# Gate values in two blocks of 512 columns, the norm weights' row spread by TensorE, and the head's steps in a new order

## The chip, the cores and the metric

The kernel runs on one core of a Trainium2 chip. The metric is device time in microseconds (us), the median of the runs. The profile is that of one execution, with every instruction's start and length; its engines are PE (TensorE matmul), PEld (its weight loads), DVE (VectorE), ACT (ScalarE), POOL (GpSimd) and SP, which only issues transfers.

## The reference

Two layers on x of 1024 tokens by 1024, all float32. The first is a chunked spatial gate, the second a Mamba-2 mixer, then a last norm. The change lies in the first layer, up to its third part v:

```python
hn = rmsnorm(h, norm_w[0])                        # h: 1024 x 1024
z, u, v = jnp.split(hn @ w_in, 3, axis=-1)        # w_in: 1024 x 6144, each part 2048 wide
v = layernorm(v, ln_w, ln_b)
mixed = jnp.einsum('gts,bcsgd->bctgd', w_causal, v.reshape(..., 8, 256)) + b_s   # 8 groups of 256 columns
h = h + (u * mixed * jax.nn.silu(z)) @ w_out
```

## The kernel before

Every float32 matmul is made of three on split operands: a value is rounded to `fp32r` (the high half, made by ACT as a rule), the rest is the low half (made by DVE), and `mm3` (lines 134 to 136) adds high x high, high x low and low x high into one accumulator in PSUM. Products of 1024-deep matrices are made by a scheme of Strassen's kind: x's transpose is cut into four quarters A11, A12, A21, A22 of 512 by 512, a block of weights into b[kh, j], and seven products replace eight. Besides quarters they take sums of them: of x S1 to S4 (lines 398 to 431), of the weights t1 = b01 - b00, t2 = b11 - t1, b10 - t2 and b11 - b01.

`Block` is one such block of weights. For the gate values v (`v_block`, line 328) a block is two groups of 256 columns (j = 0, 1), so there are four blocks; the stationary operand is a 128x128 piece of x's quarter, the moving one 256 columns of weights, and a product is two units of two halves of 4 x 3 matmuls. `done` adds what was kept of earlier products (`u`), writes 128 x 2 x 256 to `v_d` in DRAM and takes the layer norm's statistics (`bn_stats`).

`head` (line 351) is the start. Its order is written out by hand (`tc.manual_schedule`): each engine does its instructions in the order in which the code names them. For each of x's eight rows of 128 tokens: load (`load_x`), sum of squares on ACT (`sq`), the root (`rs_a`, a power on POOL; `rs_b`, a correction on DVE), scale and norm weights on DVE (`norm`, line 381; the weights `nwb` are loaded broadcast to 128 partitions), eight transposes on TensorE (`tr`, 387), and then copies and halves. Between them stand the seven products of the first block (`blk.mm`) and the start of the second. Sums of x rows are made on DVE (`sums(V, ...)`) or by a transfer through POOL's queue that adds into its target (`sums(None, ...)`, `blk.add`).

Behind the head the rest of the second block, the mixing weights (lines 560 to 586: transposes of `ws`, a matmul with `ones`) and blocks three and four follow, ordered by a scheduler. Small loads (`hv`, `dsk`, lines 594 to 606) stand in the code behind them; the scheduler put them early. `dsk` is read in single values: 64 copies of 16 values that lie two apart, twice. Then eight groups g of z and u follow (`Block` with 512 moving columns of x), whose first matmul is the first one that reads as `acc<-hh,wh`. Tiles come from pools with a fixed number of slots: `s8` 16, `q4` 8, `k2` 4 (the outputs `vt` and the mixing weights `wc` share them), `wr` 4, `wh` and `wl` 3; a tile waits until its slot is free.

Of the kernel before, what the change touches and what calls it, by code (L numbers as in the profile page):

```python
# [8 lines left out]
F32 = mybir.dt.float32  # L9
# [13 lines left out]
G = 8  # L23
# [6 lines left out]
def kernel(  # L30
# [297 lines left out]
    def v_block(gp):  # L328
        def done(name, i, a, b):
            th, j = int(name[1]) - 1, int(name[2]) - 1  # L330
            g = 2 * gp + j
            vt = k2([P, 2, 256], "vt")
            vf = vt.rearrange("p a b -> p (a b)")
            if b is None:
                nc.scalar.copy(out=vf, in_=a)
            else:
                nc.vector.tensor_tensor(out=vf, in0=a, in1=b, op=ALU.add)
            t0 = th * 4 + 2 * i
            for q in range(2):
                nc.vector.bn_stats(out=stats[:, t0 + q, g, :], in_=vt[:, q, :])  # L340
# [10 lines left out]
    def head():  # L351

        blk = v_block(0)
        V, S = nc.vector, nc.scalar
        TTv, MINUS = V.tensor_tensor, ("S1", "S2")
        rows, F, TP, ss, rs = {}, {}, {}, {}, {}
# [6 lines left out]
        def sq(t):  # L363
            if t % 2 == 0:
                ss[t] = tiny([P, 8], "ss")
            S.activation(side[:, 0], rows[t], AF.Square, accum_out=ss[t // 2 * 2][:, t % 2:t % 2 + 1])

        def rs_a(t):
            v = ss[t][:, 0:2]
            V.tensor_scalar(v, v, 1.0 / D, NORM_EPS, ALU.mult, ALU.add)  # L370
            ss[t + 1] = rsqrt_a(v, 2)

        def rs_b(t):
            r = tiny([P, 8], "rs")
            rsqrt_b(r[:, 0:2], ss[t][:, 0:2], ss[t + 1], 2)
            rs[t], rs[t + 1] = r[:, 0:1], r[:, 1:2]

        def norm(t):
            for kh in (0, 1) if t < 4 else (1, 0):
                xh = rows[t][:, kh * 512:(kh + 1) * 512]  # L380
                V.scalar_tensor_tensor(xh, xh, rs[t], nwb[kh], ALU.mult, ALU.mult)
# [1774 lines left out]
```

## Time and profile before

| | us |
|---|---|
| median of 3 runs (1493.01 to 1494.26) | 1493.28 |
| the profiled execution | 1493.6 |
| its span | 1491.9 |
| PE busy | 1452.7 (97%) |
| DVE busy | 1047.2 (70%) |
| ACT busy | 780.4 (52%) |
| POOL busy | 398.6 (27%) |

A row of the order of time gives start, length, engine, line, operation, tiles written and read, shape, count, and in brackets the idle time before and what ended it. A row of the waits gives engine, tile and line that waited, for what, the total, how often and the longest. A row of a group of instructions gives shape and count, then busy time and mean length in ns, then idle time before them. A row of transfers gives count, size and the median time from issue to landing.

### The profile page before, as it was taken

The page shows a single profiled execution, that of the slowest core. Times are in us where ns is not written, and L with a number is a line of the kernel's source. Part 1 is how long each engine was busy: PE and PEld are TensorE (multiplying, and loading weights), DVE is VectorE, ACT ScalarE, POOL GpSimd, SP SyncE. Part 2 cuts the span into 40 slices and gives each one's busy share as a digit, 9 for nine tenths or more (in the row PEclk, how much of TensorE's full clock was granted, in tenths as well). Part 3 has the DMA queues.
Part 4 walks back from the last instruction along what each step waited for, and adds up shares of the span by engine and source line. Part 5 has one row for each costly group of instructions (what it writes and reads, how often), then busy time and mean ns, then how long its engine had stood idle before and what let it go on. Part 6 is the DMA issues. An engine that isn't in the chain of part 4 may idle for free. (4 is left out here: it accounts for less than half of the span.)

```text
span 1491.9 us, 21273 instructions
## 1 busy us (share of the span) xinstructions
PE 1452.7 (97%) x7834; PEld 1225.7 (82%) x7834; DVE 1047.2 (70%) x1713; ACT 780.4 (52%) x1256; POOL 398.6 (27%) x451
## 2 busy tenths in 40 slices
PE   6899999999999999999999999999999999999997
PEld 6799988888888888887787888888888888887875
DVE  7966567766666655678764648777787777788976
ACT  6533232323233344555656646657777766866463
POOL 1111110000000023202123323204687666742221
PEclk9999999999999999999999999999999999999999
DMA  5554323333233799976476888876776675699963
GB/s 186 142 170 142 101 94 114 105 104 104 66 110 119 274 279 258 255 170 154 116 175 140 188 163 169 165 233 180 202 193 189 175 202 134 191 283 278 268 121 113
DMA packets 174953, 254.46 MB, mean 171 GB/s; under 512 B 16401, under 2 KB 103169, under 8 KB 171649
## 3 DMA queue, kind: packets, MB, share of 16 engines
q1 hardware_dynamic: 124768, 168.93, 37.0%
q0 software_dynamic: 42448, 70.27, 23.6%
q10 hardware_dynamic: 7632, 13.90, 2.6%
q8 instruction: 62, 1.02, 0.3%
q14 instruction: 43, 0.34, 0.1%
HBM read 186.14 MB, written 51.18 MB: 159 GB/s over the span
## 5 line engine op out<-in xcount | busy, mean ns | idle before, releaser
L134 PE MATMUL acc<-hh,wh 128*128 128x512 f32 x868 | 339.9, 392 | 1.3 <-ACT u L296 0.8
L136 PE MATMUL acc<-hh,wl 128*128 128x512 f32 x868 | 338.5, 390 | 1.0 <-DVE wl L112 0.9
L135 PE MATMUL acc<-hl,wh 128*128 128x512 f32 x868 | 337.8, 389 | 0.0
L112 DVE TENSOR_TENSOR wl<-wr,wh 128x1024 fp32r<-128x1024 f32 (+1 forms) x96 | 114.4, 1193 | 119.5 <-ACT wh L111 119.3
L136 PEld LDWEIGHTS acc<-hh,wl 128*128 128x128 f32 x868 | 162.9, 188 | 36.8 <-DVE wl L112 2.7
L134 PEld LDWEIGHTS acc<-hh,wh 128*128 128x128 f32 x868 | 163.1, 188 | 35.7 <-ACT u L296 1.8
L135 PEld LDWEIGHTS acc<-hl,wh 128*128 128x128 f32 x868 | 163.0, 188 | 33.1
L296 ACT COPY u<-acc 128x512 f32<-128x512 f32 x115 | 66.8, 583 | 197.8 <-PE acc L136 197.7
L111 ACT CAST wh<-wr 128x1024 fp32r<-128x1024 f32 (+1 forms) x112 | 115.1, 1028 | 94.9 <-PE acc L135 58.5
L136 PE MATMUL acc<-wh,hl 128*128 128x256 f32 x448 | 128.0, 286 | 6.0 <-DVE hl L407 4.5
L134 PE MATMUL acc<-wh,hh 128*128 128x256 f32 x448 | 128.6, 287 | 3.0 <-ACT hh L398 1.1
L135 PE MATMUL acc<-wl,hh 128*128 128x256 f32 x448 | 127.5, 285 | 1.3 <-DVE wl L421 1.3
L134 PE MATMUL ab<-hh,wh 128*128 128x512 f32 x288 | 122.2, 424 | 0.0
L136 PE MATMUL ab<-hh,wl 128*128 128x512 f32 x288 | 113.2, 393 | 0.0
L135 PE MATMUL ab<-hl,wh 128*128 128x512 f32 x288 | 112.4, 390 | 0.0
L136 PEld LDWEIGHTS acc<-wh,hl 128*128 128x128 f32 x448 | 86.6, 193 | 7.1 <-DVE hl L407 5.1
L134 PEld LDWEIGHTS acc<-wh,hh 128*128 128x128 f32 x448 | 86.6, 193 | 4.0 <-ACT hh L400 1.3
L135 PEld LDWEIGHTS acc<-wl,hh 128*128 128x128 f32 x448 | 86.7, 193 | 1.7 <-DVE wl L421 1.5
L649 POOL DMA_DIRECT2D y_d<-y x8 | 4.4, 549 | 290.3 <-DVE y L646 290.3
L1622 ACT ACTIVATE wl<-wl,tk 128x128 f32<-128x128 f32 x256 | 81.6, 392 | 0.1
L112 DVE TENSOR_TENSOR wl<-t,wh 128x1024 fp32r<-128x1024 f32 (+1 forms) x38 | 45.5, 1196 | 47.5 <-ACT wh L111 47.5
L112 DVE TENSOR_TENSOR xl<-ya,xh 128x1024 fp32r<-128x1024 f32 x36 | 44.8, 1244 | 37.2 <-ACT xh L111 35.5
(314 smaller groups left out, 3194.8 us busy)
## 6 DMA issues: line engine op xcount, KB each, us to landing
wr<-in_a_w_in_dram SPq DMA_DIRECT2D x48, 512.0 KB, 3.7
wl<-cs_d SPq DMA_DIRECT2D x64, 256.0 KB, 5.7
wr<-in_b_w_in_dram SPq DMA_DIRECT2D x30, 512.0 KB, 7.1
wb<-in_a_w_out_dram SPq DMA_DIRECT2D x10, 1024.0 KB, 12.0
wb<-in_b_w_out_dram SPq DMA_DIRECT2D x10, 1024.0 KB, 8.2
wr<-in_b_w_in_dram SPq DMA_DIRECT2D x36, 256.0 KB, 6.2
v<-v_d SPq DMA_DIRECT2D x8, 1024.0 KB, 5.5
y_d<-y POOLq DMA_DIRECT2D x8, 1024.0 KB, 5.7
```

The costliest lines, as they stand in the source:

```text
L111: nc.scalar.copy(out=hi, in_=src)
L112: return (eng or nc.vector).tensor_tensor(out=lo, in0=src, in1=hi.bitcast(F32), op=ALU.subtract)
L134: nc.tensor.matmul(out=o, lhsT=l[0], rhs=r[0], start=start, stop=False, **kw)
L135: nc.tensor.matmul(out=o, lhsT=l[0], rhs=r[1], start=False, stop=False, **kw)
L136: nc.tensor.matmul(out=o, lhsT=l[1], rhs=r[0], start=False, stop=stop, **kw)
L296: nc.scalar.copy(out=self.u[n][:, i], in_=a)
L649: store = lambda: nc.gpsimd.dma_start(out=y_d[-1], in_=y)
L1622: nc.scalar.activation(wl[:, j, :], wl[:, j, :], AF.Relu, scale=-1.0, bias=tokc(2, c, self.g)[:, j:j + 1])
```

## The change

Gate values are made in two blocks of 512 columns (`Wide`): a product is four units i of 128 tokens, each in two halves h of 2 x 3 matmuls with 512 moving columns, and the halves of different units and products are mixed. The weights are loaded in halves of 256 rows. In the first block t2 and t1 are made with transfers that add through POOL's queue: t2 from a second load of b00, to which b11 - b01 is added, and t1 in b00's own place. x's four sums of the third kind, made on DVE before, go that way beside the four of the fourth.

The norm weights arrive as one row of 4 KB, through ACT's queue; two matmuls with a row of ones spread it over 128 partitions in PSUM (`spread`). The first two rows of x are multiplied by the weights alone (`weigh`), and their scale is put on a diagonal (`diag`) that stands in for the identity in their transposes; these are then plain float32 matmuls. Ten matmuls of the identity with itself stand around the spreading (`busy`). The other six rows are made as before, half by half.

`v_d` has one tile for two groups, and an output is two pieces of 1 KB per partition. `hv` and `dsk` are loaded at the end of the head. The rest of the second block and the mixing weights are now in a hand-written order as well (`rest`).

New functions stand here as they are now, the rest cut to a few places:

```diff
-    nwb = [k2([P, 512], "nwb") for _ in range(2)]
+    nwb_ = q4([P, D], "nwb")
+    nwb = [nwb_[:, 0:512], nwb_[:, 512:1024]]
...
-    v_d = [dr.tile([P, NT, 256], F32, name=f"v_d{g}") for g in range(G)]
+    v_d = [dr.tile([P, 2, NT, 256], F32, name=f"v_d{g}") for g in range(G // 2)]
+    class Wide:
+        def __init__(self, g0):
+            self.c0, self.g0 = 2 * DI + g0 * 256, g0
+            self.b, self.Y, self.u, self.o, self.vt = {}, {}, {}, {}, {}
+            self.seventh = False
+        def rows(self, kh, j, h):
+            r0 = kh * 512 + h * 256
+            return a_w_in[r0:r0 + 256, self.c0 + j * 512:self.c0 + (j + 1) * 512].rearrange("(k p) n -> p k n", p=P)
+        def load(self, kh, j, pool, *parts):
+            if (kh, j) not in self.b:
+                if pool is s8:
+                    both = s8([P, 4, 512], "wide")
+                    self.b[kh, j] = [both[:, 0:2], both[:, 2:4]]
+                else:
+                    self.b[kh, j] = [pool([P, 2, 512], "wide") for _ in range(2)]
+            for h in parts or (0, 1):
+                nc.sync.dma_start(out=self.b[kh, j][h], in_=self.rows(kh, j, h))
+        def src(self, n):
+            b = self.b
+            return b["t2"] if n == 6 else b[{1: (0, 0), 5: (0, 0), 2: (1, 0), 4: (1, 0), 7: (0, 1), 3: (1, 1)}[n]]
+        def minus(self, dst, x, y, h):
+            b = self.b
+            nc.vector.tensor_tensor(out=b[dst][h], in0=b[x][h], in1=b[y][h], op=ALU.subtract)
+        def hi(self, n, h, eng=nc.scalar.copy, room=None):
+            self.Y[n, h] = room or (wh([P, 2, 512]), wl([P, 2, 512]))
+            eng(out=self.Y[n, h][0], in_=self.src(n)[h])
+        def lo(self, n, h):
+            h_, l_ = self.Y[n, h]
+            nc.vector.tensor_tensor(out=l_, in0=self.src(n)[h], in1=h_.bitcast(F32), op=ALU.subtract)
+        def prep(self, n, h):
+            self.hi(n, h), self.lo(n, h)
+        def mm(self, n, i, h, pool=acc):
+            on = {6: 1, 7: 1, 3: 5}.get(n, n)
+            if n == 7:
+                self.seventh = True
+            if n == 4 and self.seventh:
+                on = 1
+            if (on, i) not in self.o:
+                self.o[on, i] = pool("acc")
+            o = self.o[n, i] = self.o[on, i]
+            Xh, Xl = HS[("A11", "A12", "S4", "A22", "S1", "S2", "S3")[n - 1]]
+            s = slice(i * P, (i + 1) * P)
+            for k in range(2):
+                mm3(o, [Xh[:, 2 * h + k, s], Xl[:, 2 * h + k, s]], [y_[:, k, :] for y_ in self.Y[n, h]],
+                    h == 0 and k == 0 and on == n, h == 1 and k == 1, True)
+        def keep(self, n, i):
+            if n not in self.u:
+                self.u[n] = [q4([P, 2, 512], "u") for _ in range(2)]
+            nc.scalar.copy(out=self.u[n][i // 2][:, i % 2], in_=self.o[n, i])
+        def out(self, name, i, n, k, eng, now=True):
+            th, j = int(name[1]) - 1, int(name[2]) - 1
+            vt = self.vt[name, i] = k2([P, 2, 256], "vt")
+            vf = vt.rearrange("p a b -> p (a b)")
+            if k is None:
+                nc.scalar.copy(out=vf, in_=self.o[n, i])
+            else:
+                nc.vector.tensor_tensor(out=vf, in0=self.o[n, i], in1=self.u[k][i // 2][:, i % 2], op=ALU.add)
+            eng.dma_start(out=v_d[self.g0 // 2 + j][:, :, th * 4 + i, :], in_=vt)
+            if now:
+                self.stat(name, i)
+        def stat(self, name, i):
+            th, j = int(name[1]) - 1, int(name[2]) - 1
+            for q in range(2):
+                nc.vector.bn_stats(out=stats[:, th * 4 + i, self.g0 + 2 * j + q, :], in_=self.vt[name, i][:, q, :])
...
+        def weigh(t, kh):
+            TTv(out=weighed[:, t, kh * 512:(kh + 1) * 512], in0=rows[t][:, kh * 512:(kh + 1) * 512],
+                in1=spread[kh], op=ALU.mult)
+        def diag(t):
+            diags[t] = both[:, t]
+            V.tensor_scalar(diags[t], ident, rs[t], None, ALU.mult)
+        def busy(n, o):
+            for _ in range(n):
+                nc.tensor.matmul(out=o[:, 0:P], lhsT=ident, rhs=ident, start=True, stop=True)
+        def tr(t, pool):
+            TP[t] = [None, None]
+            for kh in (0, 1) if t < 4 else (1, 0):
+                tp = pool("tp")
+                for k in range(4):
+                    o, s = tp[:, k * P:(k + 1) * P], slice((kh * 4 + k) * P, (kh * 4 + k + 1) * P)
+                    if t in diags:
+                        nc.tensor.matmul(out=o, lhsT=weighed[:, t, s], rhs=diags[t], start=True, stop=True)
+                    else:
+                        nc.tensor.transpose(out=o, in_=rows[t][:, s], identity=ident)
+                TP[t][kh] = tp.rearrange("p (k t) -> p k t", k=4)
...
+        side = s8([P, 2, D], "side")
+        xp = [s8([P, 2, D], "xp") for _ in range(4)]
+        weighed, both = s8([P, 2, D], "weighed"), k2([P, 2, P], "both")
+        row = side[:, 1]
+        nc.scalar.dma_start(out=row[0:1, :], in_=norm_w[0:1, :])
+        x_ = lambda t: load_x(t, xp[t // 2][:, t % 2, :])
+        spare = [sb.tile([P, 2, 512], F32R, name="spare", tag="q4", bufs=8) for _ in range(2)]
+        t2 = A.b["t2"] = [q4([P, 2, 512], "t2") for _ in range(2)]
+        b = A.b
+        x_(0), x_(1), A.load(0, 0, s8), x_(2), x_(3), A.load(1, 0, s8), x_(4), x_(5), x_(6), x_(7)
+        A.load(0, 1, wr), A.load(1, 1, wr)
+        for h in range(2):
+            nc.sync.dma_start(out=t2[h], in_=A.rows(0, 0, h))
...
+        spread = [acc("nw") for _ in range(2)]
+        busy(4, spread[0])
+        for h in range(2):
+            nc.tensor.matmul(out=spread[h], lhsT=ones[0:1, :], rhs=row[0:1, h * 512:(h + 1) * 512],
+                             start=True, stop=True)
+        first = acc("first")
+        busy(6, first)
...
+        sq(0)
+        weigh(0, 0)
+        weigh(0, 1)
+        sq(1)
+        rs_a(0, 1)
+        weigh(1, 0)
+        weigh(1, 1)
+        S.copy(out=nwb[0], in_=spread[0])
+        rs_a(1, 1)
+        rs_b(0, 1)
+        S.copy(out=nwb[1], in_=spread[1])
+        A.hi(1, 0, V.tensor_copy)
+        diag(0)
+        A.hi(1, 1)
+        rs_b(1, 1)
+        tr(0, sm)
+        A.lo(1, 0)
+        sq(2)
+        diag(1)
+        hi("A11", 0)
+        A.lo(1, 1)
+        tr(1, acc)
+        sq(3)
+        lo("A11", 0)
+        copy(0, 1)
+        A.mm(1, 0, 0)
...
+        A.minus((0, 1), (1, 1), (0, 1), 0)
+        sq(6)
+        A.mm(1, 3, 1)
+        norm(4, 1)
+        nc.gpsimd.dma_start(out=t2[0], in_=b[0, 1][0], accum_op=ALU.add)
+        norm(4, 0)
...
+        nc.gpsimd.dma_start(out=b[0, 0][0], in_=A.rows(0, 1, 0), accum_op=ALU.add)
...
+        A.minus((1, 0), (1, 0), "t2", 0)
+        sums(None, 3, 4)
...
+        A.mm(7, 1, 0)
+        B.load(0, 0, wr)
+        A.keep(6, 3)
+        A.hi(3, 0)
...
     with tc.manual_schedule():
         second = head()
+        hv = cst.tile([P, 4], F32, name="hv")
...
+            nc.sync.dma_start(out=dsk[f * 64:(f + 1) * 64, :], in_=dskv[f].partition_broadcast(64))
...
-    for gp in range(G // 2):
-        if gp == 1:
-            second.run((2, 6, 7, 4, 5, 3))
-        elif gp:
-            v_block(gp).run()
...
+    def mix_b():
+        for h in range(2):
+            tp = sm("tp")
+            for k in range(4):
+                nc.tensor.transpose(out=tp[:, k * P:(k + 1) * P], in_=ws[:, h * 4 + k, :], identity=ident)
+            wcs.append(k2([P, 4, P], "wc"))
+            nc.scalar.copy(out=wcs[h], in_=tp.rearrange("p (k t) -> p k t", k=4))
+            nc.gpsimd.dma_start(out=wcT_d[:, 4 * h:4 * h + 4, :], in_=wcs[h])
+    def mix_c():
...
+    def rest(B):
+        G_, V = nc.gpsimd, nc.vector
+        def product(n, pools, sums=None, ahead=None):
+            for h in range(2):
+                for i in range(4):
+                    B.mm(n, i, h, pools[i])
+                    if h and n in (1, 6, 7):
+                        B.keep(n, i)
+                if not h and sums:
+                    sums()
+                if ahead:
+                    B.prep(ahead, h)
+        def minus(*abc):
+            for h in range(2):
+                B.minus(*abc, h)
+        four, mixed = [acc] * 4, [acc, acc, sm, sm]
+        mix_a()
+        product(2, mixed, ahead=6)
+        for i in range(4):
+            B.out("C11", i, 2, 1, G_)
+        minus((0, 1), (1, 1), (0, 1))
+        product(6, four, mix_b, ahead=7)
+        mix_c()
+        minus((1, 0), (1, 0), "t2")
+        product(7, four, ahead=4)
+        product(4, four, ahead=5)
+        for i in range(4):
+            B.out("C21", i, 4, None, G_)
+        product(5, mixed, ahead=3)
+        for i in range(4):
+            B.out("C22", i, 5, 7, G_)
+        product(3, mixed)
+        for i in range(4):
+            B.out("C12", i, 3, 6, G_)
+    with tc.manual_schedule():
+        rest(second)
...
-        nc.sync.dma_start(out=v, in_=v_d[g])
+        nc.sync.dma_start(out=v, in_=v_d[g // 2][:, g % 2])
```

What the new order does to three queues. DVE, from its two constants to the first low half of weights (`ss` sums of squares, `ru` and `rs` the root's correction, `nw` the spread weights in PSUM, `both` the diagonals, `wide` and `wr` weights). Before:

```order
L370 TENSOR_SCALAR ss<-ss 128x2
L150 TENSOR_TENSOR ru<-rr 128x2
L151 TENSOR_TENSOR ru<-ru,ss 128x2
L152 TENSOR_SCALAR ru<-ru 128x2
L153 TENSOR_TENSOR rs<-rr,ru 128x2
L381 SCALAR_TENSOR_TENSOR xp<-xp,rs,nwb 128x512 x4
L370 TENSOR_SCALAR ss<-ss 128x2
L418 CAST wh<-wr 128x1024
L407 TENSOR_TENSOR hl<-tp,hh 128x4x128
L421 TENSOR_TENSOR wl<-wr,wh 128x1024
```

After:

```order
L442 TENSOR_TENSOR weighed<-xp,nw 128x512 x2
L428 TENSOR_SCALAR ss<-ss 128x1
L442 TENSOR_TENSOR weighed<-xp,nw 128x512 x2
L428 TENSOR_SCALAR ss<-ss 128x1
L148 SCALAR_TENSOR_TENSOR ru<-rr,ss 128x1
L152 TENSOR_SCALAR ru<-ru 128x1
L153 TENSOR_TENSOR rs<-rr,ru 128x1
L360 CAST wh<-wide 128x1024
L447 TENSOR_SCALAR both<-ident,rs 128x128
```

The four passes over two rows have moved from behind the root to ahead of it, and each row has its own root.

POOL's queue, from the roots to the first store of gate values (`xp`, `xrow` rows of x; `t_97` and `t_98` the halves of t2; a row named DMA is the issue of a transfer). Before:

```order
L141 TENSOR_TENSOR rr<-ss,mhalf 128x2 x4
L202 DMA wr<-in_a_w_in_dram 128x4x256
L429 DMA xp<-xrow 128x512 x4
L341 DMA v_d_93<-vt 128x512 x2
L565 AFFINE_SELECT ws<-ws 128x1024
```

After:

```order
L141 TENSOR_TENSOR rr<-ss,mhalf 128x1 x2
L141 TENSOR_TENSOR rr<-ss,mhalf 128x2 x2
L611 DMA t_97<-wide 128x1024
L141 TENSOR_TENSOR rr<-ss,mhalf 128x2
L626 DMA wide<-in_a_w_in_dram 128x2x512
L630 DMA wide<-in_a_w_in_dram 128x2x512
L635 DMA t_98<-wide 128x1024
L500 DMA xp<-xp 128x512 x8
L861 AFFINE_SELECT ws<-ws 128x1024
L397 DMA v_d_80<-vt 256x1x256 x4
```

Five adding transfers have become twelve, four of them of 512 KB.

SP's queue, around `hv` and `dsk`. Before, between the small parameters and the first block's first stores:

```order
L453 DMA prow_101<-in_b_conv_b_dram 32x128
L595 DMA hv<-in_b_dt_bias_dram 32x1
L597 DMA hv<-in_b_a_log_dram 32x1 x4
L601 DMA dsk<-in_b_d_skip_dram 64x16x1 x2
L341 DMA v_d_91<-vt 128x512 x2
L120 DMA wr<-in_a_w_in_dram 128x4x256 x4
```

After, between the first block's last stores and the first z weights:

```order
L397 DMA v_d_79<-vt 256x1x256 x3
L860 DMA ws<-in_a_w_s_dram 128x8x128
L863 DMA bsb<-in_a_b_s_dram 128x1024
L397 DMA v_d_79<-vt 256x1x256
L831 DMA hv<-in_b_dt_bias_dram 32x1
L833 DMA hv<-in_b_a_log_dram 32x1 x4
L837 DMA dsk<-in_b_d_skip_dram 64x16x1 x2
L937 DMA v<-v_d_78 128x2048
L120 DMA wr<-in_a_w_in_dram 128x4x256 x4
```

The small loads moved from the head's beginning to behind its last store, ahead of v and of the z weights.

More of the change, by code (lines that the diff above doesn't have):

```diff
@@ L370, in rs_a, with rs_b @@
             V.tensor_scalar(v, v, 1.0 / D, NORM_EPS, ALU.mult, ALU.add)
[L371 to L373 removed]
+            ss["r", t] = rsqrt_a(v, n)
+        def rs_b(t, n=2):
             r = tiny([P, 8], "rs")
[L375 to L381 removed]
@@ L383, in tr @@
-        def tr(t):
-            tp = [(sm if t in (0, 3, 5, 6) else acc)("tp") for _ in range(2)]
-            for kh in (0, 1) if t < 4 else (1, 0):
-                for k in range(4):
-                    nc.tensor.transpose(out=tp[kh][:, k * P:(k + 1) * P],
-                                        in_=rows[t][:, (kh * 4 + k) * P:(kh * 4 + k + 1) * P], identity=ident)
-            TP[t] = [a.rearrange("p (k t) -> p k t", k=4) for a in tp]
+            rsqrt_b(r[:, 0:n], ss[t][:, 0:n], ss["r", t], n)
@@ new lines, in head @@
+        hi("A11", 1)
+        hi("A12", 0)
+        lo("A11", 1)
+        copy(0, 0)
+        rs_b(2)
+        A.mm(1, 0, 1)
+        copy(1, 1)
+        hi("A12", 1)
+        lo("A12", 0)
+        copy(1, 0)
+        norm(2, 0)
+        A.mm(1, 1, 0)
+        A.hi(2, 0)
+        norm(2, 1)
+        sq(5)
+        norm(3, 1)
+        tr(2, sm)
+        lo("A12", 1)
+        A.mm(1, 1, 1)
+        hi("A11", 2)
+        norm(3, 0)
+        A.hi(2, 1, room=spare)
+        lo("A11", 2)
+        tr(3, acc)
@@ new lines, in head @@
+        rs_b(6)
+        copy(4, 0)
+        A.minus((0, 1), (1, 1), (0, 1), 1)
+        nc.gpsimd.dma_start(out=b[0, 0][1], in_=A.rows(0, 1, 1), accum_op=ALU.add)
+        hi("A22", 4)
+        A.mm(2, 2, 0)
+        copy(4, 1)
+        lo("A22", 4)
+        nc.gpsimd.dma_start(out=t2[1], in_=b[0, 1][1], accum_op=ALU.add)
+        A.mm(2, 1, 1)
+        A.minus((1, 0), (1, 0), "t2", 0)
+        sums(None, 3, 4)
+        norm(6, 1)
+        tr(5, sm)
+        A.hi(4, 0)
+        A.out("C11", 1, 2, 1, nc.sync, False)
@@ new lines, in head @@
+        A.mm(2, 2, 1)
+        copy(5, 1)
+        norm(6, 0)
+        hi("A22", 5)
+        A.lo(4, 0)
+        copy(5, 0)
+        A.mm(2, 3, 0)
+        sums(None, 3, 5)
+        lo("A22", 5)
+        norm(7, 0)
+        tr(6, sm)
+        A.out("C11", 2, 2, 1, nc.sync, False)
+        A.mm(2, 3, 1)
+        hi("A22", 6)
+        norm(7, 1)
+        copy(6, 0)
+        lo("A22", 6)
+        copy(6, 1)
+        A.mm(4, 0, 0)
+        sums(None, 3, 6)
+        A.out("C11", 3, 2, 1, nc.sync, False)
```

421 lines of the change are left out of this document (251 added, 170 removed).

## The prediction

> **What bounds the kernel now.** I read the page's span and engine rows first, then a table of stretches over the front of the program, then TensorE's waits up to 198 us, then its order of time.
>
> ```profile
> span 1491.9 us, 21273 instructions
> PE 1452.7 (97%) x7834; PEld 1225.7 (82%) x7834; DVE 1047.2 (70%) x1713; ACT 780.4 (52%) x1256; POOL 398.6 (27%) x451
> ...
> 0.00:14.30 14.30, 3.65 (x16) 3.27 (x16) 4.62 (x14) 7.64 (x14) 2.30 (x9) 1.00 0.89 280
> 14.30:56.00 41.70, 31.78 (x238) 29.97 (x238) 39.89 (x71) 27.06 (x52) 7.70 (x8) 0.96 0.51 140
> 56.00:115.00 59.00, 59.00 (x495) 59.00 (x494) 41.19 (x64) 22.00 (x33) 4.97 (x8) 1.00 0.48 152
> 118.00:198.00 80.00, 80.00 (x663) 79.52 (x663) 48.59 (x81) 23.19 (x30) 9.72 (x18) 1.00 0.36 122
> ```
>
> A stretch's row gives its length, then busy time of PE, PEld, DVE, ACT, POOL. TensorE bounds the program (97%); it idles in the first two stretches alone. In the second DVE is busy 39.89 of 41.70 us: there DVE is the bound. From 56 us on TensorE never stops, so only fewer or shorter matmuls help there. Its waits up to 198 us:
>
> ```profile
> PE tp L387 <- DVE xp L381: 9.7, 1, 9.7
> PE acc L136 <- DVE hl L407: 4.5, 3, 1.6
> PE acc L136 <- DVE hl L405: 1.6, 2, 1.4
> PE acc L135 <- DVE wl L421: 1.3, 1, 1.3
> PE acc L134 <- ACT hh L398: 1.1, 1, 1.1
> PE acc L134 <- ACT xrow L414: 1.0, 1, 1.0
> PE acc L134 <- DVE wh L418: 1.0, 1, 1.0
> PE tp L387 <- DVE vt L337: 0.5, 1, 0.5
> ```
>
> 9.7 us pass before the first transpose; the other seven rows add up to 11.0, mostly for low halves that DVE makes.
>
> The change touches the code up to the end of the gate values (the first matmul of the z/u blocks is the 197.87 row below). Behind that place the order of instructions is the same on PE, and on the others but for short pieces, so I carry the remaining 1294.0 us over unchanged and forecast where that first z matmul comes to lie.
>
> ```profile
> 28.19 1.03 PE L387 MATMUL tp<-ident,xrow 128*128 128x128 f32 x8
> 28.98 0.37 PE L134 MATMUL acc<-wh,hh 128*128 128x256 f32 x1
> ...
> 101.72 0.28 PE L135 MATMUL acc<-wl,hh 128*128 128x256 f32 x1
> ...
> 108.44 0.28 PE L134 MATMUL acc<-wh,hh 128*128 128x256 f32 x1
> ...
> 115.47 1.13 PE L579 MATMUL tp<-wc,ones 128*128 128x512 f32 x2
> 116.44 0.60 PE L574 MATMUL tp<-ident,ws 128*128 128x128 f32 x4
> ...
> 197.87 0.40 PE L134 MATMUL acc<-hh,wh 128*128 128x512 f32 x1
> ...
> 212.85 0.39 PE L134 MATMUL acc<-hh,wh 128*128 128x512 f32 x1
> ```
>
> Durations overlap, so starts count. 56 matmuls of 256 columns lie between 101.72 and 108.44: 0.120 us each. 66 of 512 columns lie between 197.87 and 212.85: 0.227 each, less than twice as much. Eight transposes take 0.79 (0.10 each), one float32 matmul of 512 columns 0.97 (two records).
>
> **The matmuls.** 4 blocks x 7 products x 2 units x 2 halves x 4 x 3 = 1344 of 256 columns become 2 x 7 x 4 x 2 x 2 x 3 = 672 of 512. 1344 x 0.120 = 161.3; 672 x 0.227 = 152.5: 8.8 us less, all on the path, since TensorE is full from 56 us on. [...]
>
> **The start.** DVE, ahead of the first matmul on x:
>
> ```profile
> 4.50 1.06 ACT L366 ACTIVATE side<-xp 128x1024 f32<-128x1024 f32 x1 [2.41 <-DMA xp<-in_x_dram]
> 7.07 0.17 DVE L370 TENSOR_SCALAR ss<-ss 128x2 f32<-128x2 f32 x1 [5.99 <-ACT side L366]
> 7.33 0.71 POOL L141 TENSOR_TENSOR rr<-ss,mhalf 128x2 f32<-128x2 f32 x1 [5.69 <-DVE ss L370]
> 9.72 3.65 PE L387 MATMUL tp<-ident,xp 128*128 128x128 f32 x16 [9.72 <-DVE xp L381]
> 13.50 0.69 DVE L418 CAST wh<-wr 128x1024 fp32r<-128x1024 f32 x1
> L407 DVE TENSOR_TENSOR hl<-tp,hh 128x512 fp32r<-128x512 f32 x12 | 7.9, 686 | 0.3 <-ACT xrow L414 0.3
> L112 DVE TENSOR_TENSOR wl<-wr,wh 128x1024 fp32r<-128x1024 f32 (+1 forms) x96 | 114.4, 1193 | 119.5 <-ACT wh L111 119.3
> ```
>
> The first two rows' scale and weights no longer stand between x and its transposes as 0.7 us passes behind the root. Four passes with the weights alone (two halves of two rows, 0.66 each, 7.9/12) run while the root is made, and the scale enters as a 128x128 diagonal. New is that they wait for the spread row: its DMA lands at 3 to 4.5 (it cannot be slower than x's first tile, 128 times its size, which ACT uses at 4.50), and the two float32 matmuls of 512 columns cost 0.97 each, or 1.9 at half clock (the sixteen transposes at 9.72 took 3.65, not 1.6, so the array starts slow). Slow, with the row at 3.3: weights in PSUM at 5.2 and 7.1, and DVE goes on: second pass 7.8, a small step and two passes and a small step 9.5, three small ones of 0.2 make the scale 10.1, the cast (0.69) 10.8, the diagonal 11.0. Fast, the same steps from x's landing at 4.5 on end at 9.1. With the row at 4.5 it is 12.2. The matmuls on the identity that now run ahead may bring the clock up on the way, so I take **10.5** for TensorE's first useful matmul. That is 0.8 later than the 9.72 of before: the start itself gains nothing. The 16 diagonal matmuls are float32: 0.97/4 = 0.24 each, 3.9 in place of 3.65.
>
> **The waits.** These are the second large term. Before, one 256-column block gave TensorE 336 x 0.120 = 40.3 us of work while DVE split all of x; now the first block gives 336 x 0.227 = 76.3 us with the same splits of x beside it.
>
> ```profile
> L381 DVE SCALAR_TENSOR_TENSOR xrow<-xrow,rs,nwb 128x512 f32<-128x512 f32 x8 | 5.6, 747 | 0.0
> L431 DVE TENSOR_TENSOR xrow<-xrow 128x512 f32<-128x512 f32 x4 | 2.7, 689 | 0.1
> L340 DVE BATCH_NORM_STATS2 stats<-vt 128x6 f32<-128x256 f32 x4 | 1.5, 419 | 0.1
> ```
>
> DVE's share to the end of the first block, with busy time over count as price: 12 norm halves x 0.70 + 28 low halves of x x 0.66 + 8 sums x 0.68 + 16 low halves of weights and 4 differences x 1.19 + 11 outputs x 0.68 + 22 statistics x 0.38 + 3 of small ones = 75 us, over 85 us of TensorE (76.3, and 9 of transposes and parameters): 88%, where it was 96%. So DVE keeps up, but not by much; walking the new order row by row with these prices I find TensorE waiting about 1 us in all (0 to 5; 5 if DVE is 10% slower than its rows). The 11.0 us go to 1.0. Next late is DVE again, at the low halves of A22 and S1.
>
> **What else moves, and its cover.** The two broadcasts of the norm row (512 KB) leave the load queue, 1 MB of the first weights enters ahead of x's third tile, and 1 MB more (a second copy of the first weights) is loaded at its end: nothing on the path until about 27 us, when the first accumulating transfer wants that copy; if it lands later, the third rival below begins. Stores of gate values go out in pieces of 1 KB in place of 2 KB; nobody waits for them but the four slots that they hold. The loads of `hv` and `dsk` go from the head's first 25 us to behind the first block's last store (about 111 us by the walk), past four loads for the second block and ahead of v's load and the first z weights; v is wanted behind z's sixth product, 40 us later, so it is covered, and ACT's wait for `hv` costs about 1 us in a stretch in which it is busy less than half.
>
> ```profile
> 17.05 0.41 PE L134 MATMUL acc<-wh,hh 128*128 128x256 f32 x1
> 20.03 0.41 PE L136 MATMUL acc<-wh,hl 128*128 128x256 f32 x1
> ...
> GB/s 0 0 0 0 0 0 0 0 0 0 0 0 0 0 0 0 0 0 0 0 0 0 0 0 0 0 0 0 0 0 0 0 0 0 0 2 62 106 198 181
> ...
> wr<-in_a_w_in_dram POOLq DMA_DIRECT2D x1, 512.0 KB, 13.0
> dsk<-in_b_d_skip_dram SPq DMA_DIRECT2D x2, 4.0 KB
> ...
> xp<-xrow POOLq DMA_DIRECT2D x4, 256.0 KB, 6.6
> ...
> ya<-ya POOLq DMA_DIRECT2D x8, 512.0 KB, 19.5
> ```
>
> The GB/s row is of 24 to 46 us in slices of 0.55: after the two `dsk` loads are issued nothing to speak of moves until 43. The first two rows are the ends of 15 matmuls at 0.213 us, half clock, 1.4 us lost.
>
> **Sum.** Before, up to 197.87: 9.7 + 161.3 + 3.65 + 48 x 0.10 = 4.8 + 2.9 (ten parameter transposes, two float32 matmuls) + 11.0 = 193.4; the remaining 4.5 are 1.4 of half clock and 3.1 of short changes between kinds. After: 10.5 + 152.5 + 3.9 + 4.8 + 2.9 + 3.1 + 1.0 = 178.7, or 19.2 less. Against the profiled execution's own 1493.6 (span 1491.9, 1.7 around it) that is 1474.4; the median of the runs, 1493.28, lies 0.3 lower: **1474**. Bounds of the unknown costs: start 9.1 to 12.2, waits 0 to 5, the 3.1 of short changes 0 to 4.5, half clock 0 to 1.4 behind the start; together 1468.5 to 1482.5.
>
> **Rivals.**
> - DVE stays the bound. For it: 88% by its rows leaves 10 us of 85, and early on it must work nearly without a gap; against it: the same splits are spread over nearly twice the TensorE time. If all 11.0 us of waits come back: 1484.
> - The `dsk` loads hold up other queues. They last about 20 us (24 to 43 above); by the walk they begin at 114, and POOL's stores of the second block's first outputs are issued at 116 to 121. If these land only after `dsk`, the slots for the mixing weights come free at 136, and their matmul, due at 130.0, starts at 137.3: 7.3, and 1.4 of half clock: 1483. For it: the weights' load of POOL issued in that stretch took 13.0. Against it: that is a transfer of twice the size, and data moved again at 43. [...]
> - The other side: the new transfers that add into a tile through POOL's queue (t2's halves, two of weights, eight of x rows) are late, and DVE, which reads their results in its strict order, stops; behind it stand the low halves that TensorE needs. By the walk t2's first half is issued at 27 and wanted at 34, the x sums follow at intervals of 2 to 4 us. With 6.6 us to landing (the row for 256 KB) or some 6 for 512 KB nothing waits over 1 us. With the 19.5 of the stage at 560 to 600 us, where such transfers queue, DVE stands 12 us for t2, 10 for the x sums of the third kind, 4 for those of the fourth, of which 24 reach TensorE: 1498, slower. It decides from about 17 us on. Against it: loads fill the bus only until 28 here.
> [...]
>
> **How the numbers follow.** Forecast 0.74; DVE bound 0.06; `dsk` 0.08; page's gap 0.02; late sums 0.10, of which 0.03 short of the turning point, 0.03 near it, 0.04 past it. 0.2% of the time is 3 us, about what a measurement tells from no change. Faster: 0.74 + 0.06 + 0.08 + 0.02 + 0.03 = 0.93; within 0.2%: 0.03; slower: 0.04. The range 1468.5 to 1484 takes in the bounds of the sum and the first, second and fourth rival; it leaves out most of the late sums.
>
> **What would show it.** The first z matmul near 178.7 instead of 197.87; TensorE's starts 0.227 apart in both blocks; DVE still over 90% busy between 14 and 56 us, but TensorE's waits behind the first matmul under 3 us; the first diagonal matmul at 9.1 to 12.2. Wrong would be: a wait of several us on DVE at the differences of weights or the x sums with a transfer behind it (third rival), one on ACT at the copy of the mixing weights (second), or a z stage that no longer runs as before.

## The result and the profile after

The changed kernel takes 1482.23 us (median, 1481.65 to 1482.93) against 1493.01 for the kernel before: a ratio of 0.9933, 95% interval 0.9922 to 0.9943. It is faster by 11 us, not by the 19 that were forecast. In the profiled execution the first z matmul starts at 187.50 us, where the forecast has 178.7 and the kernel before 197.87:

```profile
187.50 0.39 PE L134 MATMUL acc<-hh,wh 128*128 128x512 f32 x1
```

What follows it takes 1292.7 us (1294.0 before). So the miss of 8.8 us lies ahead of z. Of all executions that stand behind the times below, one (with half the pieces, 1606.66 us) ran slow, at a mean granted clock of 0.851, and is left out.

The page's span and engine rows of the changed kernel, and its stretches of time (length, busy time of PE, PEld, DVE, ACT, POOL, granted clock (1.00 is full speed, 0.50 the half clock of the text), DMA share, GB/s):

```profile
span 1480.2 us, 20005 instructions
PE 1452.0 (98%) x7202; PEld 1196.5 (81%) x7202; DVE 1041.8 (70%) x1713; ACT 784.1 (53%) x1261; POOL 404.5 (27%) x451
...
0.00:14.30 14.30, 12.32 (x41) 9.26 (x42) 7.63 (x20) 8.26 (x13) 2.58 (x9) 1.00 0.89 330
14.30:56.00 41.70, 40.74 (x212) 33.98 (x212) 36.62 (x63) 32.57 (x57) 10.31 (x11) 1.00 0.82 218
56.00:115.00 59.00, 58.72 (x260) 48.27 (x259) 44.32 (x71) 24.66 (x37) 3.44 (x4) 1.00 0.51 151
118.00:198.00 80.00, 73.16 (x316) 58.90 (x315) 47.64 (x93) 21.87 (x30) 15.86 (x21) 0.96 0.36 121
133.00:145.00 12.00, 5.16 (x12) 2.51 (x11) 1.36 (x2) 5.02 (x8) 1.10 (x2) 0.72 0.39 133
```

The second stretch, in which TensorE was busy 31.78 us of 41.70 before, is now nearly full (40.74). The fourth, which was full, has lost 6.84 us, all of it in the last row's 12 us, and the granted clock falls there to 0.72. The first row's 1.00 is no reading: the trace's clock records begin at 14.24 us, where the clock became full, and a stretch without records shows 1.00. How slow it was before is read from the matmuls' lengths: the two that spread the norm row take 3.78 us, where one like them took 0.97 at full clock. TensorE's waits up to 198 us name the place:

```profile
PE tp L877 <- ACT wc L871: 6.8, 1, 6.8
PE nw L451 <- POOL ident masks.py:199: 1.4, 1, 1.4
PE acc L135 <- DVE wl L364: 1.0, 1, 1.0
PE tp L460 <- DVE both L447: 0.6, 1, 0.6
PE acc L134 <- DVE vt L396: 0.3, 1, 0.3
```

The waits that added up to 11.0 us are down to 1.3 (third and fifth row: a low half of weights, an output, whose accumulator comes free late); the second and fourth lie ahead of the first matmul on x. The first row is new: the matmul that sums the mixing weights waits for ACT's copy of them. What ACT waited for stands in its own order of time, in brackets:

```profile
118.93 0.20 ACT L839 ACTIVATE hv<-hv 128x1 f32<-128x1 f32 x1 [1.50 <-DMA hv<-in_b_a_log_dram]
139.75 1.23 ACT L871 COPY wc<-tp 128x512 f32<-128x512 f32 x2 [20.62 <-DMA v_d<-vt]
```

ACT stood 20.62 us for stores of gate values: the copies need slots (`k2`) that the stores have to give back. These stores in the changed kernel, and all DMA between 112 and 145 us in 40 slices of 0.83 us:

```profile
L397 POOL DMA_DIRECT2D v_d<-vt x4: 690/701/729, 119.6 to 123.8; - x4
DMA to landing us min/median/max: 17.9/19.1/20.0
...
GB/s 232 273 353 376 369 138 15 0 0 0 0 0 0 0 0 0 0 0 0 0 0 0 0 0 0 0 0 0 0 0 110 303 427 248 209 5 318 318 0 0
DMA packets 4401, 3.06 MB, mean 93 GB/s; under 512 B 2480, under 2 KB 3886, under 8 KB 4398
```

Issued at 119.6 to 123.8, they land 17.9 to 20.0 us later; in the kernel before POOL's stores of this stage took 2.7 to 4.1:

```profile
L341 POOL DMA_DIRECT2D v_d<-vt x6: 542/542/560, 100.9 to 115.4; - x6
DMA to landing us min/median/max: 2.7/2.9/4.1
```

In the changed kernel next to no bytes move from 118 to 136 us, though 2480 packets of under 512 bytes run between 112 and 145: SP has just issued the two loads of `dsk`, 2048 pieces of 4 bytes. That is the prediction's second rival. TensorE's wait at the mixing weights and the half clock behind it (137.12 to 143.95, of which TensorE works 3.56 us, so 1.8 lost) make 8.6 of the 8.8 us.

### The profile page after: what moved, and what is told of

The parts are those of the page before. It is cut to its first block, busy times and chain, and to the rows that moved or that the text cites. A ratio compares the mean times of both kernels' runs of the same rounds, so it can differ in the third digit from the quotient of the medians.

```text
span 1480.2 us, 20005 instructions
## 1 busy us (share of the span) xinstructions
PE 1452.0 (98%) x7202; PEld 1196.5 (81%) x7202; DVE 1041.8 (70%) x1713; ACT 784.1 (53%) x1261; POOL 404.5 (27%) x451
## 5 line engine op out<-in xcount | busy, mean ns | idle before, releaser
L112 DVE TENSOR_TENSOR wl<-wr,wh 128x1024 fp32r<-128x1024 f32 (+1 forms) x81 | 96.2, 1188 | 105.8 <-ACT wh L111 105.6
L111 ACT CAST wh<-wr 128x1024 fp32r<-128x1024 f32 (+1 forms) x97 | 99.3, 1025 | 78.7 <-PE acc L135 58.7
L297 ACT COPY u<-acc 128x512 f32<-128x512 f32 x93 | 53.9, 582 | 148.0 <-PE acc L136 147.9
L134 PE MATMUL acc<-wh,hh 128*128 128x512 f32 x216 | 85.6, 396 | 0.3 <-DVE vt L396 0.3
L135 PE MATMUL acc<-wl,hh 128*128 128x512 f32 x216 | 84.3, 390 | 1.0 <-DVE wl L364 1.0
L136 PE MATMUL acc<-wh,hl 128*128 128x512 f32 x216 | 84.1, 389 | 0.0
L1967 DVE TENSOR_TENSOR wl<-wl,cw 128x512 f32<-128x512 f32 x64 | 61.0, 965 | 16.2 <-ACT wl L1951 15.1
L1162 PE MATMUL bo<-wl,xh 128*128 128x512 f32 x192 | 64.2, 392 | 1.3 <-DVE stats L1253 0.7
L134 PEld LDWEIGHTS ab<-hh,wh 128*128 128x128 f32 x288 | 54.4, 189 | 13.3 <-issue 5.7
L111 ACT CAST xh<-ya 128x1024 fp32r<-128x1024 f32 x36 | 37.7, 1048 | 49.8 <-PE ao L1162 35.0
```

Of the source, the lines that this page charges most:

```text
L111: nc.scalar.copy(out=hi, in_=src)
L112: return (eng or nc.vector).tensor_tensor(out=lo, in0=src, in1=hi.bitcast(F32), op=ALU.subtract)
L134: nc.tensor.matmul(out=o, lhsT=l[0], rhs=r[0], start=start, stop=False, **kw)
L135: nc.tensor.matmul(out=o, lhsT=l[0], rhs=r[1], start=False, stop=False, **kw)
L136: nc.tensor.matmul(out=o, lhsT=l[1], rhs=r[0], start=False, stop=stop, **kw)
L297: nc.scalar.copy(out=self.u[n][:, i], in_=a)
```

## The experiments

**The small pieces taken away.** `dall` gets d_skip by whole rows; the layout is made on the chip.

```
-        for f in range(2):
-            nc.sync.dma_start(out=dsk[f * 64:(f + 1) * 64, :], in_=dskv[f].partition_broadcast(64))
+        dall = cst.tile([P, 32], F32, name="dall")
+        nc.sync.dma_start(out=dall, in_=b_d_skip[0].partition_broadcast(P))
...
+        for f in range(2):
+            nc.scalar.copy(out=dsk[f * 64:(f + 1) * 64, :],
+                           in_=dall[f * 64:(f + 1) * 64].rearrange("p (c f) -> p f c", f=2)[:, f])
```

> d_skip is loaded by one transfer of whole rows of 32 values (128 pieces of 128 bytes) and laid out by two small ACT copies, in place of two transfers of 4-byte pieces. Theory (the 4-byte pieces hold POOL's stores, these hold the slots of the mixing weights, and TensorE then runs at half clock for a while): POOL's four stores at 120 to 124 us land within some 3 us, the wait of 6.8 us at the mixing weights' matmul and the half clock behind it (1.7) are gone, the first z matmul comes at 187.5 - 8.5 = 179.0, and the time is 1482.2 - 8.5 = 1473.7 (1472.5 to 1475). Rival (the stores are late for another reason, for instance because the loads of the second block's weights fill the bus): the wait stays, 1481 to 1483.

Measured: 1471.78 us, ratio to before 0.9870 (0.9855 to 0.9885); once more on another chip 1472.08, 0.9868 (0.9854 to 0.9882). Its stores of gate values, the second stretch again, the fourth and that of the wait, and its first z matmul:

```profile
L397 POOL DMA_DIRECT2D v_d<-vt x4: 690/701/729, 117.7 to 121.9; - x4
DMA to landing us min/median/max: 2.6/2.6/2.7
...
14.30:56.00 41.70, 40.93 (x205) 34.05 (x205) 38.31 (x65) 33.11 (x58) 11.40 (x13) 1.00 0.82 218
118.00:198.00 80.00, 80.00 (x355) 65.64 (x354) 53.51 (x104) 27.71 (x38) 15.52 (x21) 1.00 0.40 134
133.00:145.00 12.00, 12.00 (x53) 9.77 (x52) 8.85 (x20) 3.60 (x7) 1.08 (x2) 1.00 0.62 217
...
176.76 0.39 PE L134 MATMUL acc<-hh,wh 128*128 128x512 f32 x1
```

The stores land in 2.6 us, TensorE is full from 118 us on at full clock, and the gain over the kernel before is 20 us. The time lies 0.7 under the theory's range: z comes 10.7 us earlier than in the changed kernel, where the theory has 8.5. The wait and the half clock are 8.6 of it; 1.65 more is the start, where the clock was full sooner in this execution (see the last experiments). The two small copies cost nothing that shows.

**The small pieces left, the user of the slots moved.** The `dsk` loads stay; the mixing weights are transposed one product later.

```
-        product(6, four, mix_b, ahead=7)
-        mix_c()
+        product(6, four, ahead=7)
...
-        product(7, four, ahead=4)
+        product(7, four, mix_b, ahead=4)
+        mix_c()
```

> The d_skip loads stay as in the changed kernel; the transposes, copies and sums of the mixing weights are put one product later (inside the seventh instead of the sixth). Theory (what TensorE waits for is only the slots): POOL's four stores land as late as in the changed kernel, 139 to 142 us, but TensorE has the seventh product to do from 133.6 to 144.5, the wait of 6.8 us shrinks to under 1 and no half clock follows: 1474.5 (1473.5 to 1476.5). Rival (the small pieces slow something else as well, weights' loads or the high parts on ACT, that the wait only covers): a wait of several us elsewhere between 118 and 150 us, 1478 to 1482.

Measured: 1473.48 us, ratio 0.9879 (0.9865 to 0.9892). The stores, and TensorE's waits up to 198 us:

```profile
L397 POOL DMA_DIRECT2D v_d<-vt x4: 690/701/729, 118.0 to 122.2; - x4
DMA to landing us min/median/max: 20.6/20.9/21.7
...
PE nw L451 <- POOL ident masks.py:199: 1.4, 1, 1.4
PE acc L135 <- DVE wl L364: 0.9, 1, 0.9
PE tp L460 <- DVE both L447: 0.6, 1, 0.6
PE acc L134 <- DVE vt L396: 0.3, 1, 0.3
```

From issue to landing the stores take even longer than in the changed kernel, and no wait of TensorE follows from it. The time is at the lower end of the theory's range (1473.5 to 1476.5). With the run above this shows both links: the pieces delay the stores, and only the slots carry the delay to TensorE.

**The pieces where the kernel before has them.** The same two loads go behind the loads of parameter rows at the head's beginning; the rest is the changed kernel.

```
             nc.sync.dma_start(out=prow2[o:o + n, :], in_=ap[0].rearrange("(c p) -> c p", p=P))
+        for f in range(2):
+            nc.sync.dma_start(out=dsk[f * 64:(f + 1) * 64, :], in_=dskv[f].partition_broadcast(64))
...
-        for f in range(2):
-            nc.sync.dma_start(out=dsk[f * 64:(f + 1) * 64, :], in_=dskv[f].partition_broadcast(64))
```

> The two d_skip loads of 4-byte pieces go back to the head's beginning, behind the loads of parameter rows, about where the kernel before has them; all else as in the changed kernel. Theory (these pieces hold the transfers of every queue for some 20 us): they run from about 28 to 49 us; POOL's first adding transfer into t2, issued at 27 and landed at 32 in the kernel with d_skip by rows, lands only at about 49, DVE stops for it from 34 to 49, and TensorE behind DVE; the wait at 133 us is gone. Against 1471.8 of the kernel with d_skip by rows that gives 12 to 18 more: 1484 to 1490. This is also the price of the prediction's third rival, had it come. Rival (only transfers of the load queue itself stand behind the pieces): 1471 to 1475.

Measured: 1486.99 us, ratio 0.9973 (0.9963 to 0.9984). POOL's adding transfers into `t2`, first with the early pieces, then in the kernel with d_skip by rows; in between TensorE's longest wait up to 210 us with the early pieces:

```profile
DMA to landing us min/median/max: 19.4/20.8/22.3
...
PE acc L134 <- DVE vt L396: 12.2, 2, 11.9
```

```profile
DMA to landing us min/median/max: 5.0/7.5/10.0
```

As the theory has it: DVE stands 12.7 us for `t2`, TensorE 11.9 behind it, and the clock is at half from 43.05 to 56.71. So the change could not have left these loads where they were: there they cost 15 us, and behind the first block, where it put them, 10. The wait is the one that the third rival describes (adding transfers that land 20 us after their issue), but its cause is another: the rival had such transfers queue behind one another, here the pieces hold them.

**Twice the pieces.**

```
+        again = cst.tile([P, 16], F32, name="again")
+        for f in range(2):
+            nc.sync.dma_start(out=again[f * 64:(f + 1) * 64, :], in_=dskv[f].partition_broadcast(64))
```

> The same two loads of d_skip stand twice, the second pair into a tile that nobody reads. Theory (the time is the number of pieces): the pieces last until about 158 us instead of 138, POOL's four stores land at 159 to 162, TensorE's wait at the mixing weights' matmul grows from 6.8 to 26 to 28 us, the time from 1482 to 1501 to 1504. Rival (the stores wait for a fixed time, or for something that the first pair alone brings): wait 6 to 10 us, 1480 to 1485.

Measured, one execution: 1486.16 us. The stores, and the wait:

```profile
L397 POOL DMA_DIRECT2D v_d<-vt x4: 687/698/727, 120.7 to 124.9; - x4
DMA to landing us min/median/max: 20.2/21.7/23.4
...
PE tp L880 <- ACT wc L874: 7.6, 1, 7.6
```

The theory fails: pieces run until 159.6 us, but the stores land at 141 to 148, among them. The wait is 7.6 us, the rival's; the time is 1.2 over the rival's range. A store is not held until the last piece is through.

**Half the pieces.** Partitions 64 to 127 come by rows, the others in pieces.

```
-        for f in range(2):
-            nc.sync.dma_start(out=dsk[f * 64:(f + 1) * 64, :], in_=dskv[f].partition_broadcast(64))
+        nc.sync.dma_start(out=dsk[0:64, :], in_=dskv[0].partition_broadcast(64))
+        dall = cst.tile([P, 32], F32, name="dall")
+        nc.sync.dma_start(out=dall, in_=b_d_skip[0].partition_broadcast(P))
```

> Half of d_skip's layout (64 partitions) is loaded in 4-byte pieces, 1024 in place of 2048; the other half comes by rows of 128 bytes and a small ACT copy. Theory (a store waits for the pieces that its DMA engines have already been given, up to the 16.5 to 18.5 us seen so far, so here for half of that): POOL's stores, issued at 118 to 122 us, land at 126 to 130; TensorE, which needs their slots for the mixing weights' copies by about 131, does not wait: 1471.5 to 1473. Rival (the hold is a fixed 17 us as soon as there are such pieces): the stores land at 136 to 141, the wait of 6 to 8 us is there, 1480 to 1483.

Measured: 1473.36 us, ratio 0.9872 (0.9853 to 0.9891).

```profile
L397 POOL DMA_DIRECT2D v_d<-vt x4: 687/698/729, 120.5 to 124.7; - x4
DMA to landing us min/median/max: 9.3/10.5/11.5
```

By the medians a store lands 10 us after its issue with 1024 pieces, 17 to 21 with 2048 (the changed kernel, the one with the mixing weights later, and the next one), and 22 with 4096. So the rival's fixed 17 us is out. The theory had the stores back at 126 to 130; they were back at 132 to 134, and TensorE did not wait even so.

**The pieces issued by another queue.**

```
-            nc.sync.dma_start(out=dsk[f * 64:(f + 1) * 64, :], in_=dskv[f].partition_broadcast(64))
+            nc.scalar.dma_start(out=dsk[f * 64:(f + 1) * 64, :], in_=dskv[f].partition_broadcast(64))
```

> The two loads of d_skip in 4-byte pieces are issued by ACT's queue in place of SP's; all else as in the changed kernel. Theory (what is held is the transfers of all queues, by the pieces, whoever issues them): POOL's stores land at 138 to 142 as before, the wait of 6 to 8 us is there, 1480 to 1483. Rival (SP's queue goes ahead of POOL's, and ACT's would not): the stores land within 3 to 6 us, 1472 to 1475.

Measured: 1486.87 us, ratio 0.9972 (0.9960 to 0.9984). The first two of POOL's stores, and waits between 110 and 150 us:

```profile
L397 POOL DMA_DIRECT2D v_d<-vt x2: 709/718/727, 120.7 to 122.1; - x2
DMA to landing us min/median/max: 16.8/17.0/17.3
...
ACT hv L839 <- DMA hv<-in_b_a_log_dram: 20.1, 1, 20.1
DVE hv L840 <- ACT hv L839: 16.7, 1, 16.7
...
PE tp L869 <- DVE vt L396: 12.0, 2, 11.8
```

POOL's stores are held nearly as long (17.0 against 19.1), so the hold does not need SP's queue. The time is above the expectation, since now SP's loads of `hv` wait as well (18.4 us from issue to landing): ACT stands for them, DVE for ACT, TensorE for DVE, 11.8 us.

**The matmuls halved again.** On top of d_skip by rows, each 512-column matmul of the gate blocks is issued as two.

```
-                mm3(o, [Xh[:, 2 * h + k, s], Xl[:, 2 * h + k, s]], [y_[:, k, :] for y_ in self.Y[n, h]],
-                    h == 0 and k == 0 and on == n, h == 1 and k == 1, True)
+                for a, c in ((0, 0), (0, 1), (1, 0)):
+                    for j in (slice(0, 256), slice(256, 512)):
+                        nc.tensor.matmul(out=o[:, j], lhsT=l[a], rhs=r[c][:, j], ...)
```

> As the kernel with d_skip by rows, but each matmul of 512 columns in the two gate blocks is issued as two of 256, which is what the kernel before does. Theory (a matmul pays about 0.006 us beside its columns, so 1344 at 0.120 stand against 672 at 0.227): the z stage starts 8.8 us later than with whole matmuls, 1473.7 + 8.8 = 1482.5 (1481 to 1484). Rival (the width gives next to nothing, the gain is all in the waits that are gone): 1474 to 1476.

Measured: 1481.82 us, ratio 0.9938 (0.9925 to 0.9951), 10.0 over the kernel with whole matmuls. Start of the first product and of z, this kernel, and below the start of the first product with whole matmuls (z at 176.76, above):

```profile
16.08 0.48 PE L385 MATMUL acc<-wh,hh 128*128 128x256 f32 x2
...
188.13 0.40 PE L134 MATMUL acc<-hh,wh 128*128 128x512 f32 x1
```

```profile
14.28 0.48 PE L134 MATMUL acc<-wh,hh 128*128 128x512 f32 x1
```

From first product to z it is 172.05 against 162.48, 9.6 more; TensorE's waits there differ by 0.9, which leaves 8.7 for the width, where the sum has 8.8. A matmul so costs 2 x 0.120 - 0.227 = 0.013 us beside its columns, not the 0.006 that the expectation names. The run does not tell whether that is the matmul's own or its weight load's: each matmul has one, and PEld, busy 79.52 of 80.00 us in the fourth stretch before, is busy 65.64 with whole matmuls. The two starts differ by another 1.8 (16.08 and 14.28), for which see the clock below.

**The norm row by broadcast, rows 0 and 1 scaled whole.** On top of d_skip by rows; the ten identity matmuls now run in one go at the start, and the spreading is gone:

```
-        x_(0), x_(1), A.load(0, 0, s8), x_(2), ...
+        x_(0), x_(1)
+        for h in range(2):
+            nc.sync.dma_start(out=nwb[h], in_=norm_w[0, h * 512:(h + 1) * 512].partition_broadcast(P))
+        A.load(0, 0, s8), x_(2), ...
...
-        diag(0)
+        norm(0, 0)
+        norm(0, 1)
```

> As the kernel with d_skip by rows, but the norm weights come as before by two broadcast loads (0.5 MB, behind x's first two tiles), and rows 0 and 1 are scaled whole by DVE and transposed plainly: no spread of the row, no diagonal matmuls. Theory (at the start DVE and the loads set the pace; the 16 float32 matmuls of 0.23 us against transposes of 0.10 cost 2.1 us, the broadcast loads delay the weights by about as much): first product matmul 14 to 16 us in place of 15.93, time within 1.5 us of the kernel with d_skip by rows. Rival (the spread is a real gain, since no weight load stands behind half a megabyte): 2 to 4 us slower, with TensorE waiting for the first low halves of weights.

Measured: 1474.26 us, ratio 0.9887 (0.9873 to 0.9900), 2.5 over the kernel with d_skip by rows: the rival's size. DVE and TensorE at the start:

```profile
11.08 0.69 DVE L360 CAST wh<-wide 128x1024 fp32r<-128x1024 f32 x1 [3.44 <-DMA wide<-in_a_w_in_dram]
11.69 1.41 DVE L439 SCALAR_TENSOR_TENSOR xp<-xp,rs,nwb 128x512 f32<-128x512 f32 x2
...
12.49 1.97 PE L462 MATMUL tp<-ident,xp 128*128 128x128 f32 x8 [6.58 <-DVE xp L439]
15.46 1.97 PE L462 MATMUL tp<-ident,xp 128*128 128x128 f32 x8 [1.01 <-DVE xp L439]
17.08 0.78 PE L134 MATMUL acc<-wh,hh 128*128 128x512 f32 x1
```

The first weights land behind the half megabyte, and DVE, whose order has their cast ahead of the norm, stops for them 3.44 us; TensorE stops 6.58 and starts the products at half clock (at 18.08, 18.51 and 18.94 us, 0.43 apart in place of 0.227). The spread by TensorE is a small gain. In this order, that is: with the norm put ahead of the cast it might be smaller, which wasn't tried.

**Without the identity matmuls at the start; with a start that they fill.** Both on top of d_skip by rows: the first drops all ten calls of `busy`, the second drops the first four and makes eleven of the last six.

```
-        busy(4, spread[0])
...
-        busy(6, first)
```

```
-        busy(4, spread[0])
...
-        busy(6, first)
+        busy(11, first)
```

> As the kernel with d_skip by rows, but without the ten multiplications of the identity by itself at the start. In the traces so far the clock changes at steps of 3.41 us whose phase differs from run to run; with these multiplications it became full at 10.1, 10.7, 14.2 and 14.6 us, and the first product matmul came at 14.3 in the first two and 15.9 in the third. Theory (the identity matmuls count as work for the clock): without them the clock stays at half until a step of 3.41 us behind 10.6 is full of work, so full at 14 to 18, first product matmul at 15.9 to 17, time 1 to 3 us above the kernel with d_skip by rows (1472.8 to 1475). Rival (mostly zeros, they count for nothing): the same first product matmul and the same time within 0.7.

> As the kernel with d_skip by rows, but the first four multiplications of the identity are gone and eleven in place of six stand behind the spread of the norm row, so that they reach up to the first diagonal matmul without a gap (6.5 to about 11.2 us). Theory (the clock becomes full behind a step of 3.41 us that is filled to more than about 84%, and the gap of 0.55 us in front of the first diagonal matmul spoils the steps that hold it): full between 9.4 and 12.8 us in every run in place of 10.1 to 16.6, the first diagonal matmul up to 0.6 later, 0.5 to 1.5 us less than the kernel with d_skip by rows in the median (1470.3 to 1471.3 against 1471.8). Rival (the gap doesn't matter, the phase decides): no difference beyond 0.5.

> The kernel with d_skip by rows once more, on the same chip as the one with the filled start, for the comparison of the two: 1471.8, with the first product matmul anywhere between 14.3 and 17 us by the phase of the clock's steps.

Measured: 1472.66 us without (0.9867, 0.9847 to 0.9888), 1473.32 filled (0.9877, 0.9860 to 0.9894), 1472.08 as it was. By time the three can't be told apart; the filled one's five executions scatter from 1470.1 to 1477.6, so that its promise is not borne out. Without them the first product came at 16.40 us, within its theory's 15.9 to 17. The traces say why the start scatters. Rows of the diagonal matmuls (32 records) in the changed kernel, with d_skip by rows (two executions), without identity matmuls, and with the filled start, each in a fence of its own:

```profile
10.62 5.55 PE L460 MATMUL tp<-both,weighed 128*128 128x128 f32 x32 [0.55 <-DVE both L447]
```

```profile
10.63 3.90 PE L460 MATMUL tp<-both,weighed 128*128 128x128 f32 x32 [0.55 <-DVE both L447]
```

```profile
10.62 5.71 PE L460 MATMUL tp<-both,weighed 128*128 128x128 f32 x32 [0.54 <-DVE both L447]
```

```profile
9.94 6.71 PE L460 MATMUL tp<-both,weighed 128*128 128x128 f32 x32 [3.40 <-DVE both L447]
```

```profile
10.89 4.01 PE L460 MATMUL tp<-both,weighed 128*128 128x128 f32 x32
```

The later the clock became full (the first of the trace's clock records), the longer they took: it did at 14.24 us in the first, 10.13 in the second, 14.57 in the third, 15.98 in the fourth, 11.46 in the fifth. The second and third are one program: its diagonal matmuls begin at 10.63 and 10.62, but its first product at 14.28 in one execution and 16.09 in the other.

## Why the prediction was right or wrong

**The matmuls' width: right.** 0.227 from start to start in both blocks; 8.7 measured for the term of 8.8. The gap per matmul to which the forecast gives a chance of 0.02 (its fourth rival) no run shows; they show 0.120 us from start to start for 256 columns and 0.227 for 512.

**The start: right in place, short in size.** The first diagonal matmul came at 10.62, forecast 10.5. In part that is luck, since 10.5 was chosen between 9.1 and 12.2: the row had landed by 2.8 us (TensorE's wait for it in the kernel without identity matmuls ends at 2.79), ahead of the 3 to 4.5 of the walk, but the two spreading matmuls took 3.8 us, the walk's slow case. The 16 diagonal matmuls were costed at 3.9 us, which is what they take at full clock; in the changed kernel's trace they ran at half for most of their time and the first product came 1.65 later than in the first trace of d_skip by rows. That much is chance: it differs from execution to execution of one program (14.28 and 16.09). The sum had no term for that; it stood only among the bounds.

**The waits for DVE: right.** 1.0 forecast, 1.3 found at the low half of weights (49.17 us) and one output. DVE is busy 88% of the second stretch, not over 90%.

**Short changes between kinds: too high.** From first product to z the kernel with d_skip by rows takes 162.48 us. 152.5 for matmuls, 4.8 for transposes, 2.9 for parameters and the 1.1 of its waits leave 1.2, where the sum put 3.1.

**The waits behind the first block: the step that failed.** The term "waits 1.0" had nothing for the slots of the mixing weights; the second rival, at a chance of 0.08, came with 6.84 us of wait and 1.8 of half clock (the rival has 7.3 and 1.4), and its time of 1483 is within a microsecond of the result. The result lies within the stated range because the range took in this rival and the sum's wide bounds; the forecast of 1474 itself missed by 8, and none of the bounds was put there for this wait. I held it unlikely because I took it that POOL's stores pass the pieces, which no trace had shown. They did not, in any of the six kernels with pieces: stores landed 9.3 to 23.4 us after their issue and, with the pieces early, the adding transfers 19.4 to 22.3, where with d_skip by rows it was 2.6 to 2.7 and 5.0 to 10.0. The row that spoke for it (a POOL load of 13.0) I discounted by its size. That load was issued at 37.3 us, and the GB/s row shows nothing moving until 43: it was waiting while the pieces ran, which already pointed to a hold.

Of the difference between 178.7 and 187.50: 6.84 the wait, 1.8 the half clock behind it, 1.65 the half clock at the start, and -1.9 for the short changes; that leaves 0.4, in small parts that I did not follow up. **The rest behind z** was taken as unchanged: 1292.7 against 1294.0.

The other rivals: DVE did not stay the bound. The late sums did not come: POOL's adding transfers into `t2` took 5.0 to 10.0 us with d_skip by rows. With the pieces early they were late.

## What to carry to other kernels

In these runs 2048 pieces of 4 bytes moved 8 KB and made the stores and the adding transfers of POOL's queue land 17 to 22 us after their issue, and SP's small loads late as well (18.4 us for `hv`) when ACT issued the pieces. So count the pieces of each transfer, and load the row whole and rearrange it on the chip. When such a transfer is moved, ask what the other queues issue in its shadow and who needs what those give back; a slot that a store frees late is a wait on an engine that has nothing to do with the DMA. A row of GB/s that is zero while packets run is the sign to look for in the profile before the change.

## What the runs showed of the hardware

**How long small pieces hold a store.** 2048 pieces over 20 us (some 318 in each 3 us of the trace) are 128 for each of 16 DMA engines, if they share them evenly, or 0.15 us a piece (an estimate from this pace). A store of another queue landed 9 to 12 us after its issue with 1024 pieces ahead of it, 17 to 22 with 2048, and 20 to 23 with 4096, when it landed in the middle of them. By the medians (10.5, 17.0 to 20.9, 21.7) the step from 1024 pieces to 2048 lengthens the hold by 6.5 to 10.4 us, and that from 2048 to 4096 by 0.8 to 4.7. What sets this length no run here shows, so it stays open.

**The clock's steps.** The half clock lasted 6.83 us in the changed kernel, 10.24 with the norm row by broadcast, 13.65 with the pieces early or on ACT's queue: 2, 3 and 4 times 3.413. The moment at which the clock first became full differed from run to run (10.1 to 16.6 us with the same first 10 us of work). In the trace of the kernel before the clock records change at 13.58, 17.00, 20.41 and 1484.73 us, which is 0, 1, 2 and 431 steps of 3.413 us behind the first change; in that of the changed kernel at 14.24, 137.12, 143.95 and 1475.14, 0, 36, 38 and 428 steps. How much work in a step goes with full clock at its end the runs do not settle. Counted in steps of 3.413 back from the moment of full clock, the step with the idle 0.55 us ahead of the first diagonal matmul in it (84% busy) ended with full clock in one run (mixing weights later, at 10.73) and not in others (the changed kernel at 10.83, the halved matmuls at 11.15, d_skip by rows again at 11.16). And 3.8 us of matmuls on operands of one row (the spread, 1*128 and 1x512 in the trace, 3.44 to 7.2 us) left the clock at half in all of them, though in the first run of d_skip by rows one such step, 3.31 to 6.72, held hardly anything else, while identity matmuls alone raised it at 5.62 in the kernel with the norm row by broadcast. That the spread counts for less is thus suggested, not shown.
